# Values made with tokens on partitions, half the queries and keys from a normed input, and attention's parts set at fixed tiles

## The chip, the cores and the metric

The kernel runs on one core of one Trainium2 chip. The metric is device time in microseconds (us) of one execution; lower is better. The time before is the median of three runs.

## The reference

Two layers of a decoder trunk over 256 tokens of width 1024. Layer 0 mixes tokens by causal pooling, layer 1 by attention; each mixer is followed by a dense squared-ReLU MLP of width 4096. The change lies in layer 1's attention. With one block of 256 keys, the block choice has nothing to choose, and this is left:

```python
def moba_attention(h, w_qkv, w_o, rel_bias):
    q, k, v = jnp.split(h @ w_qkv, 3, axis=-1)          # 16 heads of 64
    ...
    logit_own = jnp.einsum('bhqd,bhkd->bhqk', qf, k_own) * scale + bias_own
    logit_own = jnp.where((dist_own >= 0)[None, None], logit_own, -jnp.inf)
    p = jax.nn.softmax(jnp.concatenate(logits, axis=-1), axis=-1)
    out = jnp.einsum('bhqk,bhkd->bhqd', p[..., top * BL:], v_own)
    ...
    return o @ w_o

def reference(...):
    c_act = jax.nn.silu(c)
    for i in range(DEPTH):
        mod = c_act @ w_mod[i] + b_mod[i]
        sh1, sc1, g1, sh2, sc2, g2 = jnp.split(mod, 6, axis=-1)
        h = modulate(rmsnorm(x, norm_mix[i]), sh1, sc1)
        y = pool_mixer(...) if i == 0 else moba_attention(...)
        x = x + g1[:, None, :] * y
        h = modulate(rmsnorm(x, norm_mlp[i]), sh2, sc2)
        x = x + g2[:, None, :] * squared_relu_mlp(h, w_up[i], w_down[i])
    return rmsnorm(x, norm_final)
```

Everything is float32.

## The kernel before

The activations lie transposed: channels on the 128 partitions, the 256 tokens along the free dimension, eight tiles `xs[k]` for 1024 channels. Every large weight is streamed once. It comes in chunks of sixteen 128x128 tiles (1 MB, the queue of SP), and each half of a chunk, eight tiles, is split into a high and a low part: ScalarE (ACT) rounds it to fp32r (`w_hi`, `split_hi`), VectorE (DVE) subtracts (`w_lo`, `split_lo`). A product of weight and input is the sum high x high + high x low + low x high. `mm_wide` does it in two matmuls where the input's high and low parts lie side by side in one 512-column operand; `mm_sum` needs three.

The query/key/value (QKV) product and the first half of the layer's up product start before their RMS norm is known. They use the input with its gain but without the norm (`unnormed`, `raws`), with two more columns for the shift, so 258 columns, and three matmuls a tile. When a tile of outputs is done, `unnormed_out` on DVE multiplies it with the norm R and sums the shift's columns, and ACT adds the shift.

The order is written out by hand. `next_tile` counts weight tiles; `later(d, fn)` issues `fn` d tiles later; every eight tiles (a step) it issues the split of the step three ahead, and `late_mods` issues halves of the modulation vectors: each is a DVE multiplication of 1024 weights by the conditioning vector with a sum (L303), two halves of 1 MB loaded on the same queue as the weights (`LATE_MODS`, `LATE_STEPS`, `load_order`). All engines run their queues in the order of issue.

The QKV product runs over 24 output tiles of eight weight tiles, 192 tiles, step 64 to step 87 of the whole kernel: queries and keys of pair 0 and 1 first, then of each next pair, followed by the values of the pair before (`QKV_SEQ`). A pair is two heads. The parts of a pair hang on each other by `later`:

- `scores` (L996): eight small matmuls, ten tiles after the keys are done;
- `logits` and maxima on DVE (L1011, L1016), `exp` on ACT (L1022), reciprocal on DVE (L1027), `normalize` on ACT (L1033);
- `transposes` of the probabilities on TensorE (PE, L1039), 25 tiles after the scores, copied out by ACT (L1041);
- `values` (L1049): the values came out with channels on partitions, so PE turns them too, and ACT copies them (L1051);
- `outputs` (L1063, L1064): probabilities times values, then the split for the next product (L1068, L1071).

Keys and values are written in reverse order of tokens, since the bias tile T runs backwards. Then comes the output product (`wo`, 64 tiles), and the second MLP.

Of the kernel before, what the change touches and what calls it, by code (L numbers as in the profile page):

```python
# [86 lines left out]
def spread(first, last, n):  # L87
# [5 lines left out]
LATE_MODS += [(1, m, j) for m in (0, 2, 4, 3, 5) for j in range(4)]  # L93
# [3 lines left out]
    + spread(STEP_DN0, STEP_QKV - 2, 12)  # L97
    + spread(STEP_QKV + 7, STEP_WO - 1, 8)
# [7 lines left out]
N_NORMED, NORMED_AT, NORMED_GAP = 16, 30, 11  # L106

# [34 lines left out]
def tile_hybrid_pool_moba(  # L142
# [115 lines left out]
    def split_lo(h, raw, hi):  # L258
        lo = split_p.tile([P, HALF * P], F32R, tag="wlo", name=f"w{h}_lo")
        nc.vector.tensor_sub(lo, raw, hi.bitcast(F32))  # L260
        if h % 2 == 1:
            issue()
        ready.extend((hi[:, t * P : (t + 1) * P], lo[:, t * P : (t + 1) * P]) for t in range(HALF))
# [10 lines left out]

# [428 lines left out]
    def next_tile():  # L703
# [17 lines left out]
        return ready.popleft()  # L721

# [241 lines left out]

    class Pair:
        def __init__(self, p):
            self.p = p
            self.qk = None
            self.mx, self.sm, self.rs, self.PT, self.v = {}, {}, {}, {}, None


        def dst(self, j):
            p = self.p
            if self.qk is None:
                self.qk = al_tile([P, 2, S], f"qk{p}")
            if j == 2:
                self.vT = tmp.tile([P, S], F32, tag="vT", name=f"vT{p}")
                return self.vT[:, ::-1]
            return self.qk[:, 0] if j == 0 else self.qk[:, 1, ::-1]

        def done(self, j, b):
            u, e = unnormed_out(b, R[0], f"qkv{self.p}_{j}")
            later(1, lambda: nc.scalar.activation(self.dst(j), u, AF.Identity, bias=e))
            if j == 1:
                later(10, self.scores)
            if j == 2:
                later(9, self.values)

        def scores(self):
            p = self.p  # L990
            self.sc = [bank(f"sc{p}_{e}") for e in range(2)]
            for t in range(2):
                n = (t + 1) * P
                for e in range(2):
# [3 lines left out]
                        self.qk[rows, 1, S - n :], start=True, stop=True,  # L998
# [8 lines left out]

        def logits(self, t, e):
# [3 lines left out]
                L[:, e], self.sc[e][:, t * P : t * P + n], DH**-0.5, T[self.p][:, e, :n], op0=ALU.mult, op1=ALU.add  # L1012
# [22 lines left out]
        def transposes(self, e):  # L1035
            p = self.p
            pt = bank(f"pt{p}_{e}")
            for i, src in enumerate((self.prob[0][:, e, :], self.prob[1][:, e, P:], self.prob[1][:, e, :P])):
# [4 lines left out]
            self.have()  # L1043

        def values(self):
            p = self.p
            pv = bank(f"pv{p}")
            for t in range(2):
                nc.tensor.transpose(pv[:, t * P : (t + 1) * P], self.vT[:, t * P : (t + 1) * P], ident)  # L1049
            self.v = tmp.tile([P, 2, P], F32, tag="v2", name=f"v{p}")  # L1050
            later(1, lambda: nc.scalar.copy(self.v.rearrange("p a b -> p (a b)"), pv[:, :S]))  # L1051
            self.have()

        def have(self):
            if self.v is not None and len(self.PT) == 2:
                later(9 if self.p < NP - 1 else 5, self.outputs)
# [23 lines left out]
    banks = {}  # L1080
    for i, (n, k) in enumerate(QKV_ORDER):
        w = next_tile()
        p, j = divmod(n, 3)
        if k == 0:
            banks[n] = bank(f"qkv{p}_{j}")
        t = raws[k]
        mm_sum(banks[n][:, :LO], w, t[:, :LO], t[:, LO : LO + S], k == 0, k == KD - 1)
        if k == KD - 1:
            later(4 * (i % G_QKV) if i < G_QKV * KD else 0, lambda p=p, j=j, b=banks[n]: pairs[p].done(j, b))
# [25 lines left out]
    def normed_tile(k):  # L1115
        u = tmp.tile([P, S], F32, tag="h", bufs=2, name=f"h11_u{k}")
        t = act.tile([P, 2 * S], F32R, tag="T", bufs=NP, name=f"h11_{k}")
        sh = modv(1, 3, k)[:, k : k + 1]
        nc.vector.scalar_tensor_tensor(u, xs[k], gs11[:, k : k + 1], R[0], op0=ALU.mult, op1=ALU.mult)
        later(2, lambda: nc.scalar.activation(t[:, :S], u, AF.Identity, bias=sh))  # L1120

        def low():
            nc.vector.scalar_tensor_tensor(
                t[:, S:], u, sh, t[:, :S].bitcast(F32), op0=ALU.add, op1=ALU.subtract
            )
# [136 lines left out]
```

## Time and profile before

| | us |
|---|---|
| median of 3 runs | 542.46 (542.15 to 542.51) |
| the profiled execution | 542.71 |
| its span on the core | 540.9 |
| busy: PE, weight loads (PEld), DVE, ACT, POOL | 530.4, 486.9, 419.6, 318.6, 2.5 |

The stages by TensorE's timeline: head and pooling until 49.4, first up product until 143.3, first down product until 221.4 and its last tile until 232.8, QKV until 324.0, output product until 349.8, second up product until 441.9, second down product until 531.9, and the end. A busy time counts an instruction from its start to its end, and instructions of one engine can overlap a little, so the pace of a queue is read from start to start. PE is TensorE's matmuls, PEld its weight loads, POOL is GpSimd.

### The profile page before, as it was taken

To read this page: it belongs to the slowest core of one execution; us is meant where nothing else is said; L and a number is where in the kernel's file an instruction comes from. 1 tells how busy PE (TensorE), PEld (TensorE's weight loads), DVE (VectorE), ACT (ScalarE), POOL (GpSimd) and SP (SyncE) were. 2 spreads that over 40 slices of the span, in tenths; PEclk is the share of its full clock that TensorE was granted. 3 is DMA by queue.
4 is the path that set the end of the run, shared out by engine and by line. 5 is a ranking of instruction groups with operands and counts; after the bars stand their busy time and mean duration, and the time that the engine had idled before them with its cause. 6 is when DMAs were issued, how large, how long until landed. Compare 5 with 4: busy or idle time off the path is not lost.

```text
span 540.9 us, 10723 instructions
## 1 busy us (share of the span) xinstructions
PE 530.4 (98%) x4284; PEld 486.9 (90%) x4284; DVE 419.6 (78%) x849; ACT 318.6 (59%) x602; POOL 2.5 (0%) x18
## 2 busy tenths in 40 slices
PE   8999999999999999999999999999999999999995
PEld 7767999999988888999999999999998888888895
DVE  1857997799889899947999994778898878775542
ACT  4225337788644445446988777668996645445531
POOL 1000000000000000000000000000000000000000
PEclk9999999999999999999999999999999999999998
DMA  8999998478899989964567774354465666866002
GB/s 323 422 416 416 420 414 331 156 293 310 304 388 393 385 288 356 327 252 141 222 213 284 288 298 157 119 201 160 157 233 167 222 233 213 302 241 257 0 1 78
DMA packets 22337, 140.39 MB, mean 260 GB/s; under 512 B 2416, under 2 KB 4736, under 8 KB 5904
## 3 DMA queue, kind: packets, MB, share of 16 engines
q1 hardware_dynamic: 22048, 138.61, 68.5%
q10 hardware_dynamic: 144, 1.05, 0.5%
q8 instruction: 33, 0.54, 0.4%
q14 instruction: 16, 0.13, 0.1%
q0 software_dynamic: 96, 0.06, 0.0%
HBM read 138.64 MB, written 1.07 MB: 258 GB/s over the span
## 4 chain that ended last, share of the span: by engine, by line
PE 92%; DMA 6%; DVE 1%; ACT 0%; issue 0%; DVEq 0%; ACTq 0%
PE m1d L272 10%; PE m0d L272 10%; PE m0u L279 5%; PE m1u L272 5%; PE m0u L281 5%; PE m0u L280 5%; PE m1d L273 5%; PE m0d L273 5%; PE qkv L279 5%; PE qkv L280 4%; PE qkv L281 4%; PE m1u L279 3%; PE m1u L280 3%; DMA raw_c_sh<-in_w_mod 3%; PE m1u L281 3%; PE m1u L273 3%
## 5 line engine op out<-in xcount | busy, mean ns | idle before, releaser
L260 DVE TENSOR_TENSOR w_lo<-raw_w,w_hi 128x1024 fp32r<-128x1024 f32 x160 | 194.3, 1223 | 53.0 <-ACT w_hi L250 52.3
L250 ACT CAST w_hi<-raw_w 128x1024 fp32r<-128x1024 f32 x159 | 164.8, 1045 | 64.4 <-PE m1d L272 19.9
L272 PE MATMUL m1d<-m1u_al,w_hi 128*128 128x512 f32 x224 | 78.7, 394 | 0.0
L272 PE MATMUL m0d<-m0u_al,w_hi 128*128 128x512 f32 x224 | 78.1, 392 | 0.0
L303 DVE SCALAR_TENSOR_TENSOR raw_m<-raw_m,cact 128x1024 f32<-128x1024 f32 x64 | 77.7, 1218 | 0.0
L279 PE MATMUL m0u<-h,w_hi 128*128 128x256 f32 x248 | 69.8, 281 | 0.0
L281 PE MATMUL m0u<-h,w_lo 128*128 128x256 f32 x248 | 69.6, 281 | 0.0
L280 PE MATMUL m0u<-h,w_hi 128*128 128x256 f32 x248 | 69.4, 280 | 0.0
L273 PE MATMUL m1d<-m1u_al,w_lo 128*128 128x256 f32 x224 | 63.0, 281 | 0.0
L273 PE MATMUL m0d<-m0u_al,w_lo 128*128 128x256 f32 x224 | 62.8, 280 | 0.0
L279 PE MATMUL qkv<-h_raw,w_hi 128*128 128x258 f32 x192 | 57.4, 299 | 0.0
L280 PE MATMUL qkv<-h_raw,w_hi 128*128 128x256 f32 x192 | 54.5, 284 | 0.0
L281 PE MATMUL qkv<-h_raw,w_lo 128*128 128x258 f32 x192 | 54.4, 283 | 0.0
L272 PEld LDWEIGHTS m1d<-m1u_al,w_hi 128*128 128x128 f32 x224 | 42.1, 188 | 9.9
L272 PEld LDWEIGHTS m0d<-m0u_al,w_hi 128*128 128x128 f32 x224 | 42.0, 188 | 9.5
L279 PEld LDWEIGHTS m0u<-h,w_hi 128*128 128x128 f32 x248 | 46.7, 188 | 0.6 <-issue 0.4
L281 PEld LDWEIGHTS m0u<-h,w_lo 128*128 128x128 f32 x248 | 46.7, 188 | 0.2 <-DVE w_lo L260 0.2
L280 PEld LDWEIGHTS m0u<-h,w_hi 128*128 128x128 f32 x248 | 46.7, 188 | 0.0
L272 PE MATMUL m1u<-h,w_hi 128*128 128x512 f32 x128 | 44.4, 394 | 0.0
L273 PEld LDWEIGHTS m1d<-m1u_al,w_lo 128*128 128x128 f32 x224 | 42.1, 188 | 0.0
L273 PEld LDWEIGHTS m0d<-m0u_al,w_lo 128*128 128x128 f32 x224 | 42.1, 188 | 0.0
L279 PEld LDWEIGHTS qkv<-h_raw,w_hi 128*128 128x128 f32 x192 | 36.4, 190 | 3.7 <-issue 3.7
(198 smaller groups left out, 1044.4 us busy)
## 6 DMA issues: line engine op xcount, KB each, us to landing
raw_w<-in_w_all SPq DMA_DIRECT2D x79, 1024.0 KB, 5.5
raw_m<-in_w_mod SPq DMA_DIRECT2D x32, 1024.0 KB, 6.8
raw_c_sh<-in_w_mod SPq DMA_DIRECT2D x8, 1024.0 KB, 14.0
raw_c_g<-in_w_mod SPq DMA_DIRECT2D x4, 1024.0 KB, 12.6
raw_c_mlp<-in_w_mod SPq DMA_DIRECT2D x2, 1024.0 KB, 11.6
raw_c_shift<-in_w_mod SPq DMA_DIRECT2D x2, 1024.0 KB, 9.1
T<-bd SPq DMA_DIRECT2D x8, 256.0 KB, 8.8
x<-in_xT ACTq DMA_DIRECT2D x1, 1024.0 KB, 6.0
```

Of the source, the lines that this page charges most:

```text
L250: nc.scalar.copy(hi, raw)
L260: nc.vector.tensor_sub(lo, raw, hi.bitcast(F32))
L272: nc.tensor.matmul(b, hi, hl[:, : 2 * S], start=start, stop=False)
L273: nc.tensor.matmul(b[:, S:], lo, hl[:, :S], start=False, stop=stop)
L279: nc.tensor.matmul(dst, hi, xh, start=start, stop=False)
L280: nc.tensor.matmul(dst[:, :S], hi, xl, start=False, stop=False)
L281: nc.tensor.matmul(dst, lo, xh, start=False, stop=stop)
L303: nc.vector.scalar_tensor_tensor(raw[:, a], raw[:, a], 1.0, cact, op0=ALU.mult, op1=ALU.mult, accum_out=dst[:, a : a + 1])
```

## The change

1. **Order of the product.** QKV is worked in two halves. Each has the queries and keys of four pairs (64 tiles), then the values of these four pairs (32 tiles).
2. **A normed input.** From tile 29 on, every six tiles, `qkv_normed` makes one of eight tiles with norm, gain and shift: two operations on POOL, the high part on ACT six tiles later, the low part on DVE ten tiles later. The queries and keys of pairs 4 to 7 use it with `mm_wide`; ACT and DVE then only add the two halves of the bank.
3. **Values with tokens on partitions.** `values_of` holds the normed input still and streams the weights, 512 columns wide: per four weight tiles, six matmuls, for two blocks of 128 tokens. Two ACT copies of 512 columns bring the values of four pairs to SBUF. The transposes of values (L1049), their copies and their removal by `unnormed_out` are gone.
4. **Fixed tiles.** Scores and outputs of each pair are issued at tiles given in `SCORES_AT` and `OUTPUTS_AT`. The transposes stay 25 tiles behind the scores.
5. **Modulation.** One more of the late loads moves into the first down product (13 and not 12), seven and not eight are spread over the QKV stage and a little of the next; shift and gain of the MLP come in pairs of tiles, and `before_mlp1` takes the gain by pairs.
6. **Reversal.** Keys and values are no longer reversed; the bias tile is read backwards.

```diff
-QKV_SEQ = [(0, 0), (0, 1)]
-for _p in range(1, NP):
-    QKV_SEQ += [(_p, 0), (_p, 1), (_p - 1, 2)]
-QKV_SEQ += [(NP - 1, 2)]
-QKV_ORDER = k_major_first([3 * p + j for p, j in QKV_SEQ], KD, G_QKV)
+QKV_ORDER = []
+for _h in range(2):
+    _qk = [3 * p + j for p in range(4 * _h, 4 * _h + 4) for j in range(2)]
+    QKV_ORDER += k_major_first(_qk, KD, 0 if _h else G_QKV)
+    QKV_ORDER += [(3 * p + 2, k) for k in range(KD) for p in range(4 * _h, 4 * _h + 4)]
...
-LATE_MODS += [(1, m, j) for m in (0, 2, 4, 3, 5) for j in range(4)]
+LATE_MODS += [(1, m, j) for m in (0, 2) for j in range(4)]
+LATE_MODS += [(1, m, j) for j in range(4) for m in (4, 3)]
+LATE_MODS += [(1, 5, j) for j in range(4)]
...
-    + spread(STEP_DN0, STEP_QKV - 2, 12)
-    + spread(STEP_QKV + 7, STEP_WO - 1, 8)
+    + spread(STEP_DN0, STEP_QKV - 2, 13)
+    + spread(STEP_QKV + 8, STEP_WO + 6, 7)
...
+QKV_NORMED_AT, QKV_NORMED_GAP = 29, 6
+SCORES_AT = (46, 65, 84, 103, 122, 138, 155, 172)
+OUTPUTS_AT = (101, 108, 118, 137, 198, 203, 208, 213)
...
+    def normed_tile(k, u, sh, t, into, high_at, low_at):
+        later(high_at, lambda: nc.scalar.activation(t[:, :S], u, AF.Identity, bias=sh))
...
+    def next_block():
+        hi, lo, a = [next_columns() for _ in range(4)][0]
+        return hi[:, a : a + 4 * P], lo[:, a : a + 4 * P]
...
+    def qkv_normed(k):
+        t = al_tile([P, 2 * S], f"h10_{k}", F32R)
+        u = tmp.tile([P, S], F32, tag="h", bufs=2, name=f"h10_u{k}")
+        nc.gpsimd.tensor_scalar_mul(u, xs[k], gs10[:, k : k + 1])
+        nc.gpsimd.tensor_mul(u, u, R[0])
+        normed_tile(k, u, modv(1, 0, k)[:, k : k + 1], t, normed, 6, 10)
+
+    for k in range(KD):
+        at(QKV_NORMED_AT + QKV_NORMED_GAP * k, lambda k=k: qkv_normed(k))
...
         def done(self, j, b):
-            u, e = unnormed_out(b, R[0], f"qkv{self.p}_{j}")
-            later(1, lambda: nc.scalar.activation(self.dst(j), u, AF.Identity, bias=e))
-            if j == 1:
-                later(10, self.scores)
-            if j == 2:
-                later(9, self.values)
+            if j == 0:
+                self.qk = al_tile([P, 2, S], f"qk{self.p}")
+            dst = self.qk[:, j]
+            if self.p < NP // 2:
+                u, e = unnormed_out(b, R[0], f"qkv{self.p}_{j}")
+                later(1, lambda: nc.scalar.activation(dst, u, AF.Identity, bias=e))
+            else:
+                u = tmp.tile([P, S], F32, tag="u", bufs=5, name=f"qkv{self.p}_{j}_u")
+                nc.scalar.activation(u, b[:, S:], AF.Copy)
+                later(2, lambda: nc.vector.tensor_add(dst, b[:, :S], u))
...
+    def values_of(h):
+        b = [bank(f"v{h}_{t}") for t in range(2)]
+        for k in range(KD):
+            hi, lo = next_block()
+            for t in range(2):
+                own = slice(t * P, (t + 1) * P)
+                xh, xl = normed[k][:, :S][:, own], normed[k][:, S:][:, own]
+                nc.tensor.matmul(b[t], xh, hi, start=k == 0, stop=False)
+                nc.tensor.matmul(b[t], xh, lo, start=False, stop=False)
+                nc.tensor.matmul(b[t], xl, hi, start=False, stop=k == KD - 1)
+        v = values[h] = [al_tile([P, 4 * P], f"v{h}_{t}_sb") for t in range(2)]
+
+        def out(t):
+            nc.scalar.copy(v[t], b[t])
+
+        for t in range(2):
+            later(t, lambda t=t: out(t))
```

Three places show how the queues stand. The first is ACT where values reach SBUF. `L..` are logits and probabilities of a pair, `v` its values, `PT` transposed probabilities, `w.._hi` the high half of a step. Before, for pair 2:

```order
L1041 COPY PT2_0_3478<-pt2_0_3474 128x384
L1041 COPY PT2_1_3488<-pt2_1_3484 128x384
L250 CAST w79_hi_3520<-raw_w_39_3250 128x1024
L983 ACTIVATE qk4_3534<-qkv4_0_u_3512,qkv4_0_b_3514 128x256
L1051 COPY v2_3533<-pv2_3530 128x256
L1022 ACTIVATE L3_0_3469,sm3_0_3546<-L3_0_3469,mx3_0_3496 128x128 x2
```

In the changed kernel, at the end of the first half:

```order
L1083 COPY PT1_1_3409<-pt1_1_3405 128x384
L1064 ACTIVATE L2_0_3378,sm2_0_3418<-L2_0_3378,mx2_0_3383 128x128 x2
L1064 ACTIVATE L2_1_3379,sm2_1_3431<-L2_1_3379,mx2_1_3398 128x256
L1124 COPY v0_0_sb_3429<-v0_0_3257 128x512
L256 CAST w79_hi_3438<-raw_w_39_3162 128x1024
L1064 ACTIVATE L2_1_3379,sm2_1_3431<-L2_1_3379,mx2_1_3398 128x256
L1124 COPY v0_1_sb_3430<-v0_1_3258 128x512
L1075 ACTIVATE L2_0_3378<-L2_0_3378,rs2_0_3421 128x128 x2
```

The copies of values now stand between the exps of pair 2 and behind a high half.

The second is DVE in the same stretch: `mx` is the maximum that an exp waits for, `h10` the normed input, `raw_m` a modulation half. In the changed kernel:

```order
L266 TENSOR_TENSOR w77_lo_3358<-raw_w_38_2967,w77_hi_3356 128x1024
L497 SCALAR_TENSOR_TENSOR h10_7_3301<-h10_u7_3302,mod1_0_120,h10_7_3301 128x256
L1052 SCALAR_TENSOR_TENSOR L2_0_3378<-sc2_0_3372,T2_2018 128x128
L1052 SCALAR_TENSOR_TENSOR L2_0_3378<-sc2_1_3373,T2_2018 128x128
L1058 TENSOR_REDUCE mx2_0_3383<-L2_0_3378 128x2
L1052 SCALAR_TENSOR_TENSOR L2_1_3379<-sc2_0_3372,T2_2018 128x256
L308 SCALAR_TENSOR_TENSOR raw_m_1_4_1_3050,mod1_4_124<-raw_m_1_4_1_3050,cact_107 128x1024
L266 TENSOR_TENSOR w78_lo_3395<-raw_w_39_3162,w78_hi_3393 128x1024
L1052 SCALAR_TENSOR_TENSOR L2_1_3379<-sc2_1_3373,T2_2018 128x256
L1058 TENSOR_REDUCE mx2_1_3398<-L2_1_3379 128x2
```

Before, a pair's logits and maxima stood together, behind the modulation half and the low half:

```order
L303 SCALAR_TENSOR_TENSOR raw_m_1_4_2_3140,mod1_4_124<-raw_m_1_4_2_3140,cact_107 128x1024
L260 TENSOR_TENSOR w78_lo_3447<-raw_w_39_3250,w78_hi_3445 128x1024
L1011 SCALAR_TENSOR_TENSOR L3_0_3469<-sc3_0_3463,T3_2056 128x128
L1071 TENSOR_TENSOR ol1_3479<-po1_3453,ol1_3479 128x256
L1011 SCALAR_TENSOR_TENSOR L3_0_3469<-sc3_1_3464,T3_2056 128x128
L1016 TENSOR_REDUCE mx3_0_3496<-L3_0_3469 128x2
L1011 SCALAR_TENSOR_TENSOR L3_1_3470<-sc3_0_3463,T3_2056 128x256
L1011 SCALAR_TENSOR_TENSOR L3_1_3470<-sc3_1_3464,T3_2056 128x256
L1016 TENSOR_REDUCE mx3_1_3507<-L3_1_3470 128x2
```

Now the last logit and maximum of pair 2 stand behind a modulation half and a low half that came between them and the first.

The third is ACT at the end of the second half, from the exps of pair 7 on; before, this stretch lay beside the output product, with the copy of pair 7's values ahead of most of its normalisations:

```order
L1029 ACT_TABLE_LOAD
L1029 ACTIVATE warm_102<-ones_98 128x1
L250 CAST w92_hi_4247<-raw_w_46_3960 128x1024
L1033 ACTIVATE L7_0_4149<-L7_0_4149,rs7_0_4230 128x128
L1051 COPY v7_4257<-pv7_4254 128x256
L1033 ACTIVATE L7_0_4149<-L7_0_4149,rs7_0_4230 128x128
```

In the changed kernel:

```order
L1083 COPY PT6_1_3938<-pt6_1_3934 128x384
L1064 ACTIVATE L7_0_3898,sm7_0_3940<-L7_0_3898,mx7_0_3905 128x128
L1064 ACTIVATE L7_1_3899,sm7_1_3952<-L7_1_3899,mx7_1_3921 128x256
L256 CAST w90_hi_3955<-raw_w_45_3744 128x1024
L1064 ACTIVATE L7_1_3899,sm7_1_3952<-L7_1_3899,mx7_1_3921 128x256
L1071 ACT_TABLE_LOAD
L1071 ACTIVATE warm_102<-ones_98 128x1
L1075 ACTIVATE L7_0_3898<-L7_0_3898,rs7_0_3944 128x128 x2
L1075 ACTIVATE L7_1_3899<-L7_1_3899,rs7_1_3960 128x256 x2
L1124 COPY v1_0_sb_3979<-v1_0_3828 128x512
L256 CAST w91_hi_3987<-raw_w_45_3744 128x1024
L1124 COPY v1_1_sb_3980<-v1_1_3829 128x512
```

The two copies of the second values stand behind all normalisations of pair 7 and the table load.

## Rows read from the trace of the kernel before

**Rows 1.** Busy by stage: us, PE, PEld, DVE, ACT, POOL, clock, DMA share, GB/s.
```profile
143.30:221.40 78.10, 78.10 (x450) 68.57 (x449) 70.57 (x120) 37.98 (x55) 0.00 (x0) 1.00 0.95 355
232.80:324.00 91.20, 91.20 (x756) 84.81 (x755) 79.30 (x186) 68.42 (x163) 0.00 (x0) 1.00 0.66 237
```
**Rows 2.** TensorE's timeline, start of the QKV stage: start us, us, instruction.
```profile
232.88 0.29 PE L279 MATMUL qkv<-h_raw,w_hi 128*128 128x258 f32 x1
...
238.66 0.50 PE L398 MATMUL n_rms<-ones,n_acc 128*128 128x1 f32 x4
...
248.68 0.28 PE L279 MATMUL qkv<-h_raw,w_hi 128*128 128x258 f32 x1
```
**Rows 3.** TensorE's timeline, second half of the second up product.
```profile
419.85 0.40 PE L272 MATMUL m1u<-h,w_hi 128*128 128x512 f32 x1
420.08 0.28 PE L273 MATMUL m1u<-h,w_lo 128*128 128x256 f32 x1
...
424.70 0.40 PE L272 MATMUL m1u<-h,w_hi 128*128 128x512 f32 x1
```
**Rows 4.** The chain of waits in the QKV stage: start us, us added, what.
```profile
250.29 0.86 PE sc L996 x8
251.15 0.32 PE qkv L279
...
253.15 0.22 PE pv L1049 x2
...
262.70 0.33 PE pt L1039 x3
```
**Rows 5.** Groups of instructions on POOL: busy us, mean ns, idle before.
```profile
L509 POOL MEMSET win<- 128x16 f32 x6 | 0.3, 101 | 0.0
...
L241 POOL MEMSET brow<- 16x127 f32 x1 | 0.2, 193 | 0.0
```
**Rows 6.** DVE's timeline, QKV stage, and one low part at the output product.
```profile
250.56 1.23 DVE L260 TENSOR_TENSOR w_lo<-raw_w,w_hi 128x1024 fp32r<-128x1024 f32 x1 [1.12 <-ACT w_hi L250]
...
262.22 1.22 DVE L303 SCALAR_TENSOR_TENSOR raw_m<-raw_m,cact 128x1024 f32<-128x1024 f32 x1
...
263.56 1.22 DVE L260 TENSOR_TENSOR w_lo<-raw_w,w_hi 128x1024 fp32r<-128x1024 f32 x1
...
264.83 0.47 DVE L1011 SCALAR_TENSOR_TENSOR L<-sc,T 128x128 f32<-128x128 f32 x2
...
267.05 0.42 DVE L473 TENSOR_TENSOR qkv_u<-qkv,n_R 128x256 f32<-128x256 f32 x1
...
267.45 1.22 DVE L303 SCALAR_TENSOR_TENSOR raw_m<-raw_m,cact 128x1024 f32<-128x1024 f32 x1
...
268.59 1.22 DVE L260 TENSOR_TENSOR w_lo<-raw_w,w_hi 128x1024 fp32r<-128x1024 f32 x1
269.73 0.16 DVE L1027 RECIPROCAL rs<-sm 128x2 f32<-128x2 f32 x1
...
342.24 0.48 DVE L462 SCALAR_TENSOR_TENSOR h_raw<-x,gs,h_raw 128x256 fp32r<-128x256 f32 x1 [0.81 <-ACT h_raw L461]
```
**Rows 7.** ACT's timeline, QKV stage.
```profile
254.57 1.28 ACT L1022 ACT_TABLE_LOAD   x1
...
258.99 0.69 ACT L1033 ACTIVATE L<-L,rs 128x128 f32<-128x128 f32 x2
...
266.63 1.04 ACT L250 CAST w_hi<-raw_w 128x1024 fp32r<-128x1024 f32 x1
267.56 0.51 ACT L1033 ACTIVATE L<-L,rs 128x256 f32<-128x256 f32 x1
267.97 0.50 ACT L983 ACTIVATE qk<-qkv_u,qkv_b 128x256 f32<-128x256 f32 x1
268.37 0.36 ACT L1051 COPY v<-pv 128x256 f32<-128x256 f32 x1
268.63 0.41 ACT L1022 ACTIVATE L<-L,mx 128x128 f32<-128x128 f32 x1
...
270.39 0.47 ACT L1041 COPY PT<-pt 128x384 f32<-128x384 f32 x1
```

More of the change, by code (lines that the diff above doesn't have):

```diff
@@ L262, in split_lo @@
             issue()
-        ready.extend((hi[:, t * P : (t + 1) * P], lo[:, t * P : (t + 1) * P]) for t in range(HALF))
+        ready.extend((hi, lo, t * P) for t in range(HALF))
     def split(h):
@@ L485, in residual_sum, with low @@
         nc.vector.scalar_tensor_tensor(xs[k], src, gate[:, k : k + 1], xs[k], op0=ALU.mult, op1=ALU.add)
+    def normed_tile(k, u, sh, t, into, high_at, low_at):
+        later(high_at, lambda: nc.scalar.activation(t[:, :S], u, AF.Identity, bias=sh))
+        def low():
+            nc.vector.scalar_tensor_tensor(
+                t[:, S:], u, sh, t[:, :S].bitcast(F32), op0=ALU.add, op1=ALU.subtract
+            )
+            into[k] = t
+        later(low_at, low)
     rms = Rms("n0")
@@ L963, in tile_hybrid_pool_moba, with at @@
     norm_tail(rms, R, N2_AT)
+    qkv0 = now[0]
+    def at(t, fn):
+        assert t >= now[0] - qkv0, (t, now[0] - qkv0)
+        later(t - (now[0] - qkv0), fn)
+    normed = [None] * KD
+    def qkv_normed(k):
[6 more added lines that the diff above has]
+        at(QKV_NORMED_AT + QKV_NORMED_GAP * k, lambda k=k: qkv_normed(k))
     class Pair:
@@ L1042, in transposes @@
             self.PT[e] = PT
[L1043 to L1056, printed above, removed]
         def outputs(self):
@@ L1060, in outputs @@
             po = bank(f"po{p}")
+            v = values[p // 4]
             for e in range(2):
-                cols = slice(e * DH, (e + 1) * DH)
-                nc.tensor.matmul(po[cols, :S], self.v[:, 1, cols], self.PT[e][:, :S], start=True, stop=False)
-                nc.tensor.matmul(po[cols, P:S], self.v[:, 0, cols], self.PT[e][:, S:], start=False, stop=True)
+                a = p % 4 * P + e * DH
+                out = slice(e * DH, (e + 1) * DH)
+                nc.tensor.matmul(po[out, :S], v[0][:, a : a + DH], self.PT[e][:, :S], start=True, stop=False)
+                nc.tensor.matmul(po[out, P:S], v[1][:, a : a + DH], self.PT[e][:, S:], start=False, stop=True)
             def split_o():
@@ L1078, in tile_hybrid_pool_moba @@
     ol = [None] * NP
     pairs = [Pair(p) for p in range(NP)]
[L1080 to L1089, printed above, removed]
+    for h in range(2):
+        banks = {}
+        for i, (n, k) in enumerate(QKV_ORDER[h * 12 * KD : h * 12 * KD + KD * KD]):
+            w = next_tile()
+            p, j = divmod(n, 3)
+            if k == 0:
+                banks[n] = bank(f"qkv{p}_{j}")
+            if h == 0:
+                t = raws[k]
+                mm_sum(banks[n][:, :LO], w, t[:, :LO], t[:, LO : LO + S], k == 0, k == KD - 1)
+            else:
+                mm_wide(banks[n], w, normed[k], k == 0, k == KD - 1)
+            if k == KD - 1:
+                later(4 * (i % G_QKV) if h == 0 and i < G_QKV * KD else 0, lambda p=p, j=j, b=banks[n]: pairs[p].done(j, b))
+        values_of(h)
@@ L1113, in tile_hybrid_pool_moba, with normed_at @@
     normed = [None] * KD
[L1115 removed]
+    def normed_at(k):
+        t = act.tile([P, 2 * S], F32R, tag="T", bufs=NP, name=f"h11_{k}")
         u = tmp.tile([P, S], F32, tag="h", bufs=2, name=f"h11_u{k}")
[L1117 to L1118 removed]
         nc.vector.scalar_tensor_tensor(u, xs[k], gs11[:, k : k + 1], R[0], op0=ALU.mult, op1=ALU.mult)
[L1120 to L1125, printed above, removed]
[L1126 to L1128 removed]
+        normed_tile(k, u, modv(1, 3, k)[:, k : k + 1], t, normed, 2, 6)
     for k in range(KD):
[L1131 removed]
+        later(NORMED_AT + NORMED_GAP * k, lambda k=k: normed_at(k))
     al = up(1, raws, R, normed)
```

36 lines of the change are left out of this document (17 added, 19 removed).

## The prediction

> **What bounds the kernel now.** I read the busy times by stage first, then TensorE's own timeline, then the chain of waits, and last the queues of VectorE (DVE) and ScalarE (ACT) inside the query/key/value (QKV) stage. In that stage TensorE is busy for 91.20 of 91.20 us at a granted clock of 1.00, the upper of its two levels, while DVE is busy for 79.30 and ACT for 68.42 [rows 1]. So nothing but TensorE's own slots sets the time there, and the two others have 12 and 23 us left over. The reader should take two things from this: a slot taken off TensorE is worth its whole length only as long as DVE and ACT keep delivering in time, and DVE, at 87%, has little room for a burst. Slots are read from starts, since the printed durations overlap: 16 tiles (48 matmuls) run from 232.88 to 238.66, so a tile of three matmuls takes 0.361 us [rows 2]. In the second half of the last up product, where the input is already normed, a tile is a 512-column and a 256-column matmul: 14 tiles from 419.85 to 424.70 are 0.346 each, 0.23 of it the 512 columns [rows 3]. The chain of waits runs over TensorE through the attention parts, and gives their price: a pair's scores take 0.86 and make the first matmul behind them 0.32 instead of 0.12, so 1.06 in all; one head's transposes 0.33; the two transposes of a pair's values 0.22 [rows 4].
>
> **What comes off TensorE.** Queries and keys of pairs 4 to 7 are 64 tiles, 0.361 to 0.346: 1.0 us. The value products are 64 tiles of 0.361, 23.1 us; now they are 16 blocks of six 512-column matmuls, 96 slots. Their nearest row is the 512-column slot of 0.23, which gives 22.1 and a gain of 1.0; at twice the 0.120 of a narrow slot it would be 23.0 and a gain of 0.1. I take 1.0. Eight pairs of value transposes go: 8 x 0.22 = 1.8. Scores, transposes of probabilities and outputs keep their count. Together 3.8 us, if TensorE still waits for nothing.
>
> The 0.23 has a rule against it: the Trainium skill, page "TensorE: Matmul & The Clock Gate", section "Back-to-back issue gap", puts a warm 512-column matmul at 512/2.4 + 2.5, an estimate of 0.216 us. By it the blocks would gain 2.4 and not 1.0, and the total would be 542.7 and not 543.4, as the first block's half of the difference would only lengthen the first wait below. The rows show 0.23, and the measurement decides.
>
> **What is added beside TensorE.** Eight normed inputs: each two GpSimd (POOL) operations, one ACT and one DVE operation. ACT loses eight value copies and eight value removals for eight normed highs and four 512-column copies; DVE loses the eight value removals (0.40 each, multiplication and column sum) for eight normed lows of 0.40; for pairs 4 to 7 a plain addition takes the place of the removal. One modulation load and its two DVE halves (2.5 us) move ahead of the stage, into the first down product, where DVE has 70.57 of 78.10 busy [rows 1]. I cost that at nothing: 7.5 us of idle DVE hide it. If they don't, it is up to 2.5 us, since the split weights come late. On the DMA queue the moved load passes ahead of the weight chunks behind it; the same bound covers it. POOL has only fills in the trace: 127 elements in 0.19 us [rows 5]. For 256 elements with inputs to read that gives at least 0.39 by its length; the nearest row that reads two inputs is DVE's 0.40. I take 0.4 to 0.9 per operation, 0.8 to 1.8 per input. An input is due every six tiles, 6 x 0.361 = 2.17 us, so POOL keeps up and costs nothing.
>
> **The new waits.** This is the step that decides. Outputs and transposes now stand at fixed tiles, and both heads' worth of values of four pairs come out of PSUM through two ACT copies. The first output (tile 101, counted from the stage's start) comes five tiles behind the last value matmul. Tile 40 starts at 248.68 [rows 2], with nothing moved on TensorE before it. From there to tile 101: 24 tiles x 0.361 = 8.67, three scores x 1.06 = 3.18, four transposes x 0.33 = 1.32, 48 slots x 0.23 = 11.04, five tiles x 0.346 = 1.73; TensorE arrives at 274.6 and needs the second copy 0.15 later, at 274.8.
>
> That copy stands on ACT behind: exp of pair 2, copy, high weight half, exp of pair 2, copy. The first exp needs pair 2's last maximum, and on DVE this stands behind everything issued up to tile 89. From the low half of step 72, which starts at 250.56 [rows 6], DVE's queue to that maximum is: seven low halves x 1.14 (268.59 to 269.73), four q/k removals x 0.40 (267.05 to 267.45), seven normed lows x 0.40 (0.48 shown, less the 0.08 by which rows overlap), logits and maxima of pairs 0, 1 and 2 at 2.22 each (264.83 to 267.05), two modulation first halves x 1.14 and one second half 1.34, four reciprocals 0.3 [rows 6]: 8.0 + 1.6 + 2.8 + 6.7 + 3.6 + 0.3 = 23.0. So the maximum is there at 273.5 at the earliest. ACT's tail is two exps of 0.44 (1.76 for four), one high half of 0.93 and two copies [rows 7]. A copy of 512 columns lies between 0.26 (256 columns) and 0.93 (1024); I take half of 0.93, 0.47. That is 2.8, and 0.2 for the hand-overs between engines (an estimate): 276.5. TensorE waits at least 1.7 us. DVE will not run without a gap: its low half of step 73 needs a high half whose buffer is free only at tile 48 (248.68 + 8 x 0.361 + 1.06 = 252.6), and ACT has a normed high in front of it; this puts it at 254.4 and not at 253.2. The low half of step 75 waits some 0.5 more, since ACT first does pair 0's four normalisations. With these 1.7 us the copy is done at 278.2: a wait of **3.4 us**, of which a part may already show at the transposes of pairs 0 and 1.
>
> The second block ends the same way. From the first transposes of pair 6 ACT has, before the second copy of values: two PT copies x 0.36, four exps 1.76, two high halves 1.86, the table load 1.28, four normalisations 1.5 (0.69 for two narrow, 0.41 for a wide one), two copies 0.94 [rows 7]: 8.1, and 8.4 with 0.3 (an estimate) for the small activation behind the table load and the hand-overs. TensorE has in the same time, to the first output of pair 4: one transpose more of pair 6 and one of pair 7 0.66, 18 slots x 0.23 = 4.14, six tiles x 0.361 = 2.17, 0.15: 7.1. A wait of **1.3 us**. In between, pair 4's scores find their keys about a microsecond early, and the outputs of pairs 5 to 7 have their values lying ready.
>
> **Sum.** The profiled execution took 542.71 us, 0.25 over the median of 542.46. 542.71 - 3.8 + 3.4 + 1.3 = 543.6; on the median 543.4, against 542.46 a change of +0.9, or 0.17%. What a measurement can tell from no change here is about 0.2%, 1.1 us.
>
> **Rivals.** *The cover holds (23%).* DVE at 87% of the stage never made TensorE wait before, since each part was issued at a distance behind what it needs. For this the copy at 278.2 would have to be ready by 274.8, DVE and ACT together 3.4 us quicker over 27: other operations shorter than their rows, or the queue less closed than I read it. Then 542.46 - 3.8 = 538.7, or 540.0 with the second wait alone. Against it: the 23.0 us are a plain count of rows.
>
> *POOL and DVE collide (14%).* From tile 40 to tile 96 twelve POOL operations run beside DVE operations that read two SBUF tensors (low halves, normed lows, modulations: 14.4 of the 23.0 us). If such a DVE operation stands still while POOL runs, twelve operations of 0.4 to 0.9 cost 12 x 0.65 x 14.4/23.0 = 4.9 at the middle, 3.0 at the lower end, all of it on the queue that sets the first wait: 543.4 + 3.0 to 4.9, about 547. It decides from 0.15 us on, as the total is then over 543.55, slower by over 0.2%. For it: DVE is what the first output waits for. Against it: no row shows the two together. The Trainium skill, page "GPSIMD Engine Reference", section "Specifications", lists POOL's SBUF interfaces as shared with VectorE, with contention against instructions that have two SBUF inputs; no trace here shows it yet.
>
> *The moved modulation is not hidden (5%).* Weights late in the first down product, +2.5 less what the later stage gains: about 544.5.
>
> **How the numbers follow.** My forecast has 58%; its own range is 541.5 (both waits at their lower bounds, 1.7 and 1.2) to 545.2 (values gain only 0.1, first wait 4.3). About half of that lies within 0.2%, nearly half above. Faster: 0.23 + 0.04 = 0.27. Same: 0.28 + 0.02 = 0.30. Slower: 0.26 + 0.14 + 0.03 = 0.43. The range that leaves out no more than two in ten reaches into both rivals: 539.0 to 547.0.
>
> **What would show it.** TensorE's waits in the changed profile: one for the ACT copy of values at the first output of pair 0, 2 to 4 us, one near the end of the stage of about 1.3, little else. Start to start, value slots of 0.23; tiles of pairs 4 to 7 at 0.346; no value transposes. If TensorE has no wait, the cover held and my count of the queues is wrong. If DVE's low halves or normed lows are longer than 1.22 and 0.48 between 244 and 272 us, POOL and DVE collide. If ACT waits long for POOL, POOL is slower than 2.17 us per input.

## The result, and the profile after

The changed kernel takes **547.10 us** (median of 4, 546.93 to 548.88) against 542.44 before. It is slower by 4.7 us; the ratio of the means is 1.0094, 95% interval 1.0073 to 1.0116. The forecast was 543.4, the range 539.0 to 547.0.

The profiled execution took 547.05 us. The busy times on its page:

```profile
PE 531.4 (97%) x4108; PEld 476.9 (87%) x4108; DVE 420.7 (77%) x836; ACT 316.7 (58%) x598; POOL 18.8 (3%) x34
```

PE, DVE and ACT are as busy as before; POOL is new. The busy times by stage, columns as in [rows 1], with two short windows behind:

```profile
142.90:220.90 78.00, 78.00 (x450) 68.46 (x449) 72.41 (x122) 37.89 (x55) 0.93 (x1) 1.00 0.96 366
232.30:324.40 92.10, 89.22 (x568) 73.82 (x567) 74.08 (x158) 68.26 (x167) 15.35 (x15) 0.98 0.57 202
...
272.00:274.00 2.00, 1.88 (x9) 1.50 (x10) 1.97 (x7) 2.00 (x5) 0.00 (x0) 0.72 0.35 70
274.00:276.00 2.00, 2.00 (x6) 1.63 (x5) 2.00 (x3) 0.93 (x5) 0.00 (x0) 0.50 0.90 369
```

The first down product is 78.0 us long, as before: the modulation load moved there is hidden. In QKV, TensorE now stands idle for 2.9 us, and in the two short windows its granted clock falls from 1.00 to the lower level, 0.50. DVE is less busy than before over the whole stage (74.1 for 79.3), so its mean explains nothing. The times are lost at single places, as TensorE's waits show (us in total, times, longest):

```profile
PE pt L1081 <- ACT L L1075: 2.1, 3, 1.4
PE po L1094 <- ACT v_sb L1124: 1.5, 2, 0.8
```

TensorE's timeline at these places:

```profile
261.21 0.44 PE L1081 MATMUL pt<-vec,L 128*128 128x128 f32 x2 [0.36 <-ACT L L1075]
261.40 0.49 PE L1118 MATMUL v<-w_hi,h 128*128 128x512 f32 x1
...
269.61 0.40 PE L1120 MATMUL v<-w_hi,h 128*128 128x512 f32 x1
271.43 0.33 PE L1081 MATMUL pt<-vec,L 128*128 128x128 f32 x1 [1.42 <-ACT L L1075]
272.12 0.84 PE L1081 MATMUL pt<-vec,L 128*128 128x128 f32 x5 [0.36 <-ACT L L1075]
272.72 0.63 PE L1118 MATMUL v<-w_hi,h 128*128 128x512 f32 x1
...
276.13 0.48 PE L1120 MATMUL v<-w_hi,h 128*128 128x512 f32 x1
276.45 0.40 PE L1118 MATMUL v<-w_hi,h 128*128 128x512 f32 x1
...
278.76 0.28 PE L279 MATMUL qkv<-h,w_lo 128*128 128x256 f32 x1
278.97 0.65 PE L1093 MATMUL po<-PT,v_sb 128*64 128x256 f32 x2
280.32 0.32 PE L1094 MATMUL po<-PT,v_sb 128*64 128x128 f32 x1 [0.71 <-ACT v_sb L1124]
...
281.12 0.51 PE L278 MATMUL qkv<-h,w_hi 128*128 128x512 f32 x1
...
326.97 0.28 PE L286 MATMUL wo<-ol,w_lo 128*128 128x256 f32 x1
...
328.75 0.32 PE L1094 MATMUL po<-PT,v_sb 128*64 128x128 f32 x1 [0.78 <-ACT v_sb L1124]
...
329.55 0.55 PE L1081 MATMUL pt<-vec,L 128*128 128x128 f32 x3
...
359.83 0.52 PE L403 MATMUL n_rms<-ones,n_acc 128*128 128x1 f32 x4
361.08 0.61 PE L403 MATMUL n_rms<-ones,n_sq 128*128 128x1 f32 x4 [0.73 <-ACT n_sq L392]
```

Read from start to start, less what each part costs undisturbed: the transposes of pair 0 lose 0.75 us; those of pair 1 lose 2.2 (269.84 to 272.72, less six transposes, 0.66); behind them nine value slots run from 272.72 to 276.45, most of them 0.43 instead of 0.23, which loses 1.6; the first output loses 1.25 (278.88 to 281.12, less 1.0). That is 5.8 us in the first half. The first output of pair 4 loses 1.5 (327.09 to 329.55, less 1.0), and the sums of squares in the second up product 0.9 (359.83 to 361.08, less the 0.36 that run 3 shows below).

What stands behind the first group, on DVE, ACT and POOL:

```profile
254.00 1.41 DVE L266 TENSOR_TENSOR w_lo<-raw_w,w_hi 128x1024 fp32r<-128x1024 f32 x1 [0.92 <-ACT w_hi L256]
...
258.15 1.62 DVE L266 TENSOR_TENSOR w_lo<-raw_w,w_hi 128x1024 fp32r<-128x1024 f32 x1
...
261.01 1.21 DVE L308 SCALAR_TENSOR_TENSOR raw_m<-raw_m,cact 128x1024 f32<-128x1024 f32 x1
...
262.15 1.75 DVE L266 TENSOR_TENSOR w_lo<-raw_w,w_hi 128x1024 fp32r<-128x1024 f32 x1
...
264.67 0.48 DVE L497 SCALAR_TENSOR_TENSOR h<-h_u,mod,h 128x256 fp32r<-128x256 f32 x1
...
271.11 1.23 DVE L266 TENSOR_TENSOR w_lo<-raw_w,w_hi 128x1024 fp32r<-128x1024 f32 x1 [0.77 <-ACT w_hi L256]
...
276.56 0.69 DVE L1058 TENSOR_REDUCE mx<-L 128x2 f32<-128x512 f32 x1
```

```profile
265.78 0.51 ACT L494 ACTIVATE h<-h_u,mod 128x256 fp32r<-128x256 f32 x1 [2.02 <-POOL h_u L1003]
...
277.28 0.51 ACT L1064 ACTIVATE L<-L,mx 128x256 f32<-128x256 f32 x1 [2.35 <-DVE mx L1058]
277.79 0.56 ACT L1124 COPY v_sb<-v 128x512 f32<-128x512 f32 x1
...
279.70 0.57 ACT L1124 COPY v_sb<-v 128x512 f32<-128x512 f32 x1
...
353.29 0.51 ACT L466 ACTIVATE h_raw<-x,gs 128x256 fp32r<-128x256 f32 x1 [1.18 <-DVE gs L371]
```

```profile
248.64 0.92 POOL L1002 TENSOR_SCALAR h_u<-x,gs 128x256 f32<-128x256 f32 x1 [1.98 <-DVE h L497]
249.65 0.73 POOL L1003 TENSOR_TENSOR h_u<-h_u,n_R 128x256 f32<-128x256 f32 x1
...
260.40 1.08 POOL L1002 TENSOR_SCALAR h_u<-x,gs 128x256 f32<-128x256 f32 x1 [1.71 <-DVE rs L1069]
261.56 1.26 POOL L1003 TENSOR_TENSOR h_u<-h_u,n_R 128x256 f32<-128x256 f32 x1
262.80 1.89 POOL L1002 TENSOR_SCALAR h_u<-x,gs 128x256 f32<-128x256 f32 x1
264.78 0.97 POOL L1003 TENSOR_TENSOR h_u<-h_u,n_R 128x256 f32<-128x256 f32 x1
...
266.73 1.52 POOL L1003 TENSOR_TENSOR h_u<-h_u,n_R 128x256 f32<-128x256 f32 x1
```

Three low halves that took 1.23 before [rows 6] take 1.41 to 1.75 while POOL runs, and POOL's two operations, 0.92 and 0.73 where no such DVE operation runs beside them, grow to 1.89 and 1.52. From 260.40 to 265.75 POOL works on two inputs with hardly a pause: 5.35 us, where two take 3.3 undisturbed. ACT stands 2.0 us for the second of them, from 263.8 on. Later an exponential waits 2.35 us for pair 2's maximum. The first copy of values goes right behind it at 277.79, the second behind a high half and one more exponential at 279.70, though the last value matmul had ended by 277.3. At 353.3 an activation waits for its piece of the MLP's gain.

### The profile page after: what moved, and what is told of

It is laid out like the page before. It is cut to its first block, busy times and chain, and to the rows that moved or that the text cites. A ratio compares the mean times of both kernels' runs of the same rounds, so it can differ in the third digit from the quotient of the medians.

```text
span 545.3 us, 10363 instructions
## 1 busy us (share of the span) xinstructions
PE 531.4 (97%) x4108; PEld 476.9 (87%) x4108; DVE 420.7 (77%) x836; ACT 316.7 (58%) x598; POOL 18.8 (3%) x34
## 4 chain that ended last, share of the span: by engine, by line
PE 80%; DMA 6%; DVE 6%; ACT 6%; issue 2%; DVEq 0%; ACTq 0%
PE m1d L278 10%; PE m0d L278 9%; PE m0u L284 5%; PE m1u L278 5%; PE m0u L286 5%; PE m0u L285 5%; PE m1d L279 5%; PE m0d L279 5%; DMA raw_c_sh<-in_w_mod 3%; PE qkv L278 3%; PE m1u L279 3%; PE m1u L284 2%; PE m1u L285 2%; PE m1u L286 2%; DMA raw_c_g<-in_w_mod 2%; DVE w_lo L266 2%
## 5 line engine op out<-in xcount | busy, mean ns | idle before, releaser
L284 PE MATMUL m1u<-h_raw,w_hi 128*128 128x258 f32 x128 | 36.5, 285 | 0.0
L285 PE MATMUL m1u<-h_raw,w_hi 128*128 128x256 f32 x128 | 36.3, 284 | 0.0
L286 PE MATMUL m1u<-h_raw,w_lo 128*128 128x258 f32 x128 | 36.2, 283 | 0.0
L279 PE MATMUL m1u<-h,w_lo 128*128 128x256 f32 x128 | 35.5, 277 | 0.0
```

What stands on the lines that cost most here:

```text
L279: nc.tensor.matmul(b[:, S:], lo, hl[:, :S], start=False, stop=stop)
L284: nc.tensor.matmul(dst, hi, xh, start=start, stop=False)
L285: nc.tensor.matmul(dst[:, :S], hi, xl, start=False, stop=False)
L286: nc.tensor.matmul(dst, lo, xh, start=False, stop=stop)
```

## The experiments

The theory after this reading: the waits come from DVE's and ACT's queues in the order in which they were issued; POOL lengthens the first, and the split gain makes the last. The rivals are in the expectations. All times are medians; in brackets is the 95% interval of the ratio of the means to the kernel before, whose median was 542.4 to 542.5 each time.

**1. Fill the idle stretch.**

```diff
+            for _ in range(12 if (p, e) == (1, 0) else 0):
+                nc.tensor.matmul(pt[:, 3 * P :], ident, ident, start=True, stop=True)
             for i, src in enumerate((self.prob[0][:, e, :], ...
```

> The changed kernel with twelve 128-column matmuls on the identity, written to unused columns of the same bank, ahead of the transposes of pair 1, where TensorE stood idle from 269.8 to 271.4 us and the granted clock then fell to its lower level. If the idle stretch brought the clock down, it now stays at 1.00 in 272 to 277 us, the value slots behind it are 0.23 and not 0.43, and the time is 1.4 to 1.7 us lower than the changed kernel's 547.1: about 545.5. If the clock falls for another reason, or if it is paid elsewhere, the time stays within 0.4 of 547.1 and the slots of 0.43 remain; a later wait (first output of pair 0) may take back up to all of it if that is bound by ACT's copy of the values and not by TensorE, since TensorE would then only arrive earlier: then 546.5 to 547.1 with the clock at 1.00.

547.33 us (1.0086 to 1.0115): nothing gained. The clock did stay up (busy times and clock by window):

```profile
272.00:276.00 4.00, 4.00 (x25) 3.48 (x25) 3.96 (x9) 2.94 (x9) 0.00 (x0) 1.00 0.64 219
```

TensorE then waited at the first output instead, whose second matmul started at 280.33 as before. So without the idle stretch the clock stayed up, and the slower slots behind it don't set the time: the second copy of the values does. The waits at the transposes are not tested by this run, since the filling stood in their place.

**2. DVE in POOL's place.**

```diff
-        nc.gpsimd.tensor_scalar_mul(u, xs[k], gs10[:, k : k + 1])
-        nc.gpsimd.tensor_mul(u, u, R[0])
+        nc.vector.scalar_tensor_tensor(u, xs[k], gs10[:, k : k + 1], R[0], op0=ALU.mult, op1=ALU.mult)
```

> The changed kernel with the two POOL operations of each normed input replaced by one DVE operation of 0.40 us (8 x 0.40 = 3.2 us more on DVE). Theory POOL and DVE collide: low halves of 1.41, 1.62 and 1.75 us go back to 1.22, ACT no longer idles 2.4 us for POOL, the transposes of pair 1 wait less than 1 us instead of 2.2, the clock stays at 1.00, and the time falls by 2 to 4 us to 543 to 545. Theory plain count (DVE's queue is simply full): the 3.2 us more on DVE make the values' copy later, the wait at the first output of pair 0 grows to 3 us or more, and the time stays at 547 or rises to 549.

546.92 us (1.0075 to 1.0103), level. The low halves are 1.22 again, the transposes of pair 1 wait 0.8 and the clock stays at 1.00, as the theory of the collision said. But the transposes of pair 0 now wait 1.5, and the copies come at 277.65 and 279.56, only 0.14 earlier. Both theories were half right: POOL's disturbance costs about as much as eight more DVE operations of 0.40 us do ahead of the last maximum.

**3. The gain in one operation.**

```diff
-        if n // 2 not in gained11:
-            gained11.add(n // 2)
-            gain(1, 4, V_NMLP, gs11, n // 2 * 2, n // 2 * 2 + 2)
+        if n == 0:
+            gain(1, 4, V_NMLP, gs11)
```

> The changed kernel with the gains of the second MLP made in one operation at the first column, as before the change, instead of four on two columns each. Theory: two of ACT's scaled inputs wait for their piece of the gain (1.18 and 0.72 us), which stands on DVE behind a low half; this makes the sums of squares late, and TensorE waits 0.73 us at them in the second up product. Then the time falls by 0.6 to 0.9 us to about 546.3 and that wait is gone. Rival: the column chain is late because the output product's data are late; then the wait stays and the time is within 0.3 of 547.1.

546.54 us (1.0070 to 1.0097), 0.6 less, though the five executions lie between 546.17 and 548.07. In the timeline of the profiled one, which took 548.0, the sums of squares have no wait:

```profile
361.67 0.50 PE L403 MATMUL n_rms<-ones,n_acc 128*128 128x1 f32 x4
362.03 0.58 PE L403 MATMUL n_rms<-ones,n_sq 128*128 128x1 f32 x4
```

The edit takes this wait away, so the split gain is shown as its cause; its price is 0.9 us by the timelines and 0.6 by the medians.

The same execution shows something on the clock. Its first half is unchanged, and the transposes of pair 1 wait about as long as in the changed kernel, but the clock stays up behind them and falls later, behind 0.93 and 1.27 us of waiting at the first output (busy times and clock by window):

```profile
271.74 0.33 PE L1081 MATMUL pt<-vec,L 128*128 128x128 f32 x1 [1.46 <-ACT L L1075]
```

```profile
272.00:276.00 4.00, 3.64 (x19) 2.96 (x19) 3.97 (x9) 3.24 (x9) 0.00 (x0) 1.00 0.55 205
...
280.00:284.00 4.00, 3.37 (x16) 2.45 (x18) 1.36 (x3) 2.22 (x8) 0.00 (x0) 0.68 0.98 383
```

There no later wait hides it, and the QKV stage is 1.5 us longer than in the profiled execution of the changed kernel. So the same idle stretch doesn't bring the clock down in every execution.

**4. All transposes six tiles later, the outputs 4 to 12.** `later(31)` and `later(32)` for 25 and 26, `OUTPUTS_AT = (112, 120, 127, 143, 203, 208, 212, 218)`.

> The changed kernel with all transposes of probabilities six tiles later and the outputs at 112, 120, 127, 143, 203, 208, 212 and 218 instead of 101, 108, 118, 137, 198, 203, 208 and 213. Theory fixed tiles: the waits are the distance between the queues and the tiles that were set, 4.2 us in the first half (with 1.6 of lower clock behind them) and 1.5 at the first output of pair 4; six tiles are 2.2 us or more, so the waits at the transposes go, the clock stays at 1.00, and the time falls by 4.5 to 7 us, to 540 to 542.6, below the 542.4 of the kernel before or level with it. Theory throughput: DVE and ACT can't deliver the first half's work in its time wherever it stands; the wait moves to the next weights, scores or outputs and the time falls by less than 2 us, to 545 or more.

545.07 us (1.0035 to 1.0062): 2.0 less, between the two. The transposes no longer wait and the clock stays at 1.00, but new waits stand in TensorE's timeline:

```profile
273.46 0.50 PE L1120 MATMUL v<-w_hi,h 128*128 128x512 f32 x1 [1.25 <-DVE h L497]
...
290.86 0.93 PE L1036 MATMUL sc<-qk 64*128 64x128 f32 x8 [2.18 <-DVE qk L1027]
```

The first is a normed low part that POOL made late; the second are keys whose addition stands on DVE behind a modulation half and a low half. Placing alone gives less than half of the 4.7 us back.

**5. The copies of the values first.**

```diff
         for t in range(2):
-            later(t, lambda t=t: out(t))
+            out(t)
```

> The changed kernel with the two ACT copies of each value block issued right behind the block's last matmul, ahead of the exponentials, the high weight half and the normalisations that stand before them in ACT's queue; nothing else moves. Theory (ACT works in order: the copy is late because an exponential ahead of it waits for pair 2's maximum on DVE, at 277.2 us): both waits for the copies, 1.2 us at the first output of pair 0 and 1.4 at that of pair 4, go, and the time falls by 2.0 to 3.0 us to 544.1 to 545.1; the wait of 2.2 us at the transposes of pair 1 stays. Rival (the exponentials are what is late, and the copy only stands beside them): the exponentials come a microsecond later, the transposes or outputs of pair 2 wait in place of the first output, and the time falls by less than 1 us, to 546.1 or more.

544.81 us (1.0031 to 1.0056), 2.3 less, within the theory's 2.0 to 3.0. No matmul waits for a copy any more; at the first output of pair 4 two weight loads still do, 0.28 and 0.29 us. So the copies were not late by their own input: ACT's order put them behind exponentials that waited for DVE.

**6. Copies first and the filling.** Both edits.

> The run with the copies put first, and the twelve filling matmuls ahead of the transposes of pair 1 with it. The filling alone changed nothing (547.33), since the first output waited for the copy in any case. Theory (the lower clock costs 1.6 us in 272 to 277 us, and was hidden behind that wait): with the copies first it is no longer hidden, so that the filling now gains 1.4 to 1.7 us on the run with the copies first. Rival (the lower clock is hidden or made up elsewhere too): the two runs agree within 0.4.

543.74 us (1.0012 to 1.0030), 1.1 less than with the copies alone. In windows of the run with the copies first, and then of this one:

```profile
272.00:276.00 4.00, 3.88 (x13) 3.12 (x14) 3.96 (x9) 2.93 (x9) 0.00 (x0) 0.60 0.59 223
```

```profile
272.00:276.00 4.00, 4.00 (x26) 3.52 (x25) 3.97 (x9) 3.52 (x10) 0.00 (x0) 1.00 0.67 213
```

The lower clock costs time once nothing later hides it; where 1.4 to 1.7 was expected, it was 1.1.

**7. Modulations later.** `spread(STEP_QKV + 14, STEP_WO + 6, 7)` for `STEP_QKV + 8`.

> The changed kernel with the seven modulation loads of this stretch spread from step 14 of the QKV stage on and not from step 8: four halves of 1.14 us leave DVE's queue between tile 64 and tile 96, three of them ahead of pair 2's maximum. Theory (DVE's queue sets the copy and so the first output): the maximum comes up to 3.4 us earlier, the waits of the first half shrink by 2 to 3.4 us together, and the time falls to 543.7 to 545.1. Rival (the POOL operations and ACT's waits for them set it): the time falls by less than 1 us, to 546.1 or more, as the normed inputs are as late as before.

546.12 us (1.0054 to 1.0079), 1.0 less: outside the theory's range, on the border of the rival's. Pair 2's last maximum came at 275.17 and not 276.56, 1.4 earlier although three halves (3.4 us) had left DVE's queue ahead of it: DVE then waited for high halves, 1.0 and 1.1 us before 262.4 and 267.4, where it had been busy. DVE's queue is one part of the cause, not all.

**8. Without POOL's part.**

```diff
-        u = tmp.tile([P, S], F32, tag="h", bufs=2, name=f"h10_u{k}")
-        nc.gpsimd.tensor_scalar_mul(u, xs[k], gs10[:, k : k + 1])
-        nc.gpsimd.tensor_mul(u, u, R[0])
+        u = xs[k]
```

> The changed kernel without POOL's part of the eight normed inputs: gain and reciprocal root mean square are left out of the input of the values and of the queries and keys of pairs 4 to 7, and the high and low parts are made from the residual stream itself, so ACT's and DVE's operations keep their number and form. Theory POOL and DVE collide: the low halves of 1.41, 1.62 and 1.75 us are 1.22 again, ACT loses its waits of 0.35 and 2.02 us for POOL, and the copies of the first values come 1.1 to 2.7 us earlier: 544.4 to 546.0. Rival plain count: POOL runs beside, the copies come within 0.4 us of 277.8 and 279.7, and the time is within 0.4 of 547.1.

544.90 us (1.0037 to 1.0062), 2.2 less. From DVE's, ACT's and TensorE's timelines:

```profile
258.14 1.22 DVE L266 TENSOR_TENSOR w_lo<-raw_w,w_hi 128x1024 fp32r<-128x1024 f32 x1
...
274.34 0.69 DVE L1056 TENSOR_REDUCE mx<-L 128x2 f32<-128x512 f32 x1
...
277.49 0.57 ACT L1122 COPY v_sb<-v 128x512 f32<-128x512 f32 x1
...
278.11 0.32 PE L1092 MATMUL po<-PT,v_sb 128*64 128x128 f32 x1 [1.27 <-ACT v_sb L1122]
```

The copies come 2.2 us earlier, the low halves have their old length, and the transposes of pair 1 wait for nothing. POOL's part is worth 2.2 us. Pair 2's maximum starts at 274.34 and not 276.56, also 2.2 earlier, and the rows say how POOL had delayed it: 1.1 us is the stretch of three low halves (1.41, 1.62 and 1.75 for 1.22), and 1.1 us are two waits of DVE for ACT, 0.29 at 270.2 and 0.77 at 271.1, which come after ACT's 2.0 for POOL and are gone in this run. The run also takes away POOL's waits for its two buffers, so that the stretch alone is read from the rows and not parted by an experiment.

**9 to 12. Putting it together.** All four have the copies first, the gain in one and the modulations from step 14. Run 9 keeps POOL and sets the transposes four tiles later and the outputs at 106, 112, 122, 139, 201, 206, 210, 215; run 10 lets ACT do the scaling (`nc.scalar.activation(u, xs[k], AF.Copy, scale=gs10[:, k : k + 1])`) and POOL the norm; run 11 has DVE's single operation; run 12 is run 11 with the transposes of pairs 0 and 1 four tiles later.

> Four edits together: copies of the values first, the MLP gains in one operation, the modulations from step 14, and the transposes four tiles later with the outputs of pairs 0 to 7 at 106, 112, 122, 139, 201, 206, 210 and 215; POOL keeps its two operations. Theory (DVE's and ACT's queues, and the order in them, made every wait): 544.8 of the run with the copies first, less 0.6 for the gain, 1.5 to 1.9 for the transposes of pair 1 and 1.1 for the lower clock behind them: 541.2 to 541.6, below the 542.5 of the kernel before. Rival: the low parts of the normed inputs, which POOL makes late, become the next wait, as in the run with all parts six tiles later (1.6 us): 542.5 to 543.5.

541.85 us (0.9980 to 0.9998), 0.6 under the kernel before. This lies between the theory's range and the rival's. The normed inputs made no wait; TensorE waited 1.0 us at one pair's scores and 0.7 at transposes.

> Copies first, gains in one operation, modulations from step 14, at the tiles of the changed kernel, and the first POOL operation of each normed input (the scaling) made by ACT instead, 8 x 0.41 us. Theory POOL and DVE collide: with half of POOL's work gone about half of its 2.2 us goes, the transposes of pair 1 wait less than 0.8 us instead of 2.2, the clock stays at 1.00 behind them, and the time is 541.0 to 542.0. Rival: ACT's 3.3 us more make the normalisations late, the transposes of pairs 0 and 1 wait 2 us or more, the clock falls, and the time is 543 or more.

546.96 us (1.0067 to 1.0095): the rival, by another way than it names. TensorE waits 3.9 us at the transposes of pair 0; on ACT:

```profile
257.39 0.51 ACT L1002 ACTIVATE h_u<-x,gs 128x256 f32<-128x256 f32 x1 [2.32 <-DVE h L497]
```

The scaling now waits on ACT for one of the two `h_u` buffers, until DVE has made an earlier low part; pair 0's table load (1.28 us, from 258.31) and exponentials stand behind it.

> The same with the normed inputs' two POOL operations replaced by one DVE operation of 0.40 us, no POOL and no more ACT. With POOL alone exchanged for DVE the time stood at 546.92, as 2.8 us of DVE before the copy cost as much as POOL's 2.2; here the modulations are out of that stretch and the copies no longer stand behind the maxima. Theory (only DVE's load ahead of the normalisations of pairs 0 and 1 counts now): the transposes of pairs 0 and 1 wait 1 to 2 us together and the time is 541.0 to 542.5. Rival: DVE is short of time throughout, weights or scores wait: 543 or more.

542.16 us (0.9987 to 1.0005), as the theory said: the transposes of pair 0 wait 1.5 us, those of pair 1 not at all.

> The run with DVE's single operation, copies first, gains in one and modulations from step 14, and with the transposes of pairs 0 and 1 alone four tiles later; the outputs stay at the changed kernel's tiles. There the transposes of pair 0 still cost 1.5 us of waiting, the only wait of its QKV stage over 0.3. Theory: four tiles are 1.4 us or more, the wait goes and nothing else is near: 542.16 less 1.3 to 1.8, 540.4 to 540.9, below the 542.5 of the kernel before by 0.3%. Rival: the wait at pair 0 is what keeps TensorE from arriving early elsewhere, at the low parts of the normed inputs or the transposes of pair 1, and moves there: 541.5 to 542.2.

542.27 us (0.9981 to 0.9999): the rival, 0.1 above its range, and no gain on run 11. The wait at pair 0 shrank to 0.4, but TensorE waited elsewhere:

```profile
PE sc L1035 <- DVE rs L1068: 1.1, 2, 0.6
...
PE pt L1080 <- ACT L L1074: 0.6, 2, 0.4
```

Runs 9 and 12 are 0.1% under the kernel before, with intervals that end just short of no change. None reached the full gain of the slots.

## Why the prediction was wrong

It had the right places and counted DVE's and ACT's queues rightly, but put at nothing what then made most of the difference, POOL's part: it said "+0.9", and 4.7 was measured.

- **What comes off TensorE, 3.8: nearly right.** From the starts of all TensorE instructions of the stage, matmuls of weights and value transposes took 74.9 us before and take 71.4 after without the waits (the values from run 12, where nothing disturbed them): 3.5. A tile with the normed input is 0.347, as in [rows 3], and a value slot 0.23, as taken. By the Trainium skill's 0.216 us for a 512-column matmul (page "TensorE: Matmul & The Clock Gate", section "Back-to-back issue gap") it would have been 1.4 more; the trace does not agree. That section gives the figure for an isolated matmul, and about 0.131 us for a stream of them, which the prediction left out; the 0.23 here agrees with neither.
- **The first wait, 3.4: mis-sized, it was 5.8.** The step said that the second copy is done at 278.2, 45.3 us after the stage's start at 232.88. In the changed kernel the matmul that needs it started at 280.32, 48.0 after the start. Without POOL's part (run 8) it started at 278.11, 45.6 after 232.55. So the count of DVE's and ACT's queues held to 0.3 us, and what it left out is POOL: 2.4 us here and between the QKV stages of the two runs, 2.2 between their medians. That a part of the wait shows at the transposes was said; there it was half of it.
- **"POOL keeps up and costs nothing": the step that failed.** It took 0.8 to 1.8 us per input against one due every 2.17. Undisturbed an input takes 1.65; beside DVE two took 5.35, slower than the 2.17 each at which they were due, and ACT waited 2.0 us for POOL. POOL in turn stretched three low halves by 1.1 us. The rival *POOL and DVE collide*, given 14%, is what happened. Its price was 3.0 to 4.9 and is 2.2 to 2.4; that its total of about 547 was met is luck, since the gain, the slots and the second wait made up for the rest.
- **The lower clock: not in the sum.** It costs 1.6 us of slots. In the profiled execution of the changed kernel it is hidden behind the copy (run 1); it costs 1.1 as soon as the copy is in time (run 6), and 1.5 where it falls behind the copy (run 3).
- **The second wait, 1.3: right, 1.5.**
- **The gain in four pieces: overlooked.** Point 5 of the change names it, and the prediction gave it no term. It costs 0.9 by the timelines, 0.6 by the medians of run 3.
- **The moved modulation at nothing: right**, the first down product kept its 78.0 us.

So, by the timelines, 0.9 + 2.4 (first wait, POOL) + 0.9 (gain) + 0.3 (slots) + 0.2 (second wait) = 4.7. With the smaller prices that the medians of runs 8 and 3 give, 2.2 and 0.6, it is 4.2; the 0.5 between is of the size by which two executions differ, so the sum is not known more closely than that. The rival *the cover holds* is refuted. No run went below 541.85: in the burst from 250 to 305 us another part was late each time one was moved, normed inputs and keys in run 4, scores and transposes in runs 9 and 12.

## What to carry to other kernels

A stage whose busiest helper engine is 80 to 87% busy on the mean, as DVE here, may have no spare time where parts of several units fall together. Lay out each queue over the burst, operation by operation; here that count held to 0.3 us once POOL was out of it. Put a copy that the main engine waits for ahead of work that waits for a third engine: issuing two pairs of copies earlier gave 2.3 us. Before work is given to an idle POOL, look at what DVE does at the same time; here, doing the same work on DVE took the same time (run 2).

## What the runs showed of the hardware

POOL and DVE slow each other, but not evenly. Low halves, which read two tensors from SBUF, took 1.41 to 1.75 us instead of 1.22 beside POOL, and a POOL operation 1.89 instead of 0.92. Normed lows and modulation halves read two as well and kept their 0.48 and 1.21 (264.67 and 261.01 above). Beside them only POOL grew: its second operation took 0.97 instead of 0.73 beside a normed low and 1.52 beside a modulation half (from 266.73). In run 7, where that half was gone, the same operation took 0.74. Maxima, which read one, kept their 0.42 and 0.69. The Trainium skill, page "SBUF — State Buffer", section "Who interferes with whom", says that a DVE instruction with two SBUF inputs contends with a POOL instruction that reads SBUF. The trace agrees that the two collide, and shows that which of them is stretched differs by operation. It adds the price here, 2.2 us for eight inputs.

TensorE's granted clock fell to its lower level (1.2 GHz) at about 272.7 us, behind 1.42 and 0.36 us of idle time with one transpose between, and was up again at 276.3. The length of the idle time alone doesn't say whether it falls. It stayed at 1.00 behind 1.46 and 0.36 us at the same place in run 3, and in run 4 behind 0.30 and 1.25 us with matmuls of 512 columns around them and behind 2.18 us at the scores. What decides it, these runs do not show.
